# Sixteen weight loads moved from SyncE's to GpSimd's DMA queue, and nine small transpositions issued before the copy out of their tile, in a two-layer decoder step

## The chip, the cores and the metric

The kernel runs on one core of one Trainium2 chip. The metric is device time in microseconds of one execution. PE is TensorE, DVE is VectorE, ACT is ScalarE, POOL is GpSimd, SP is SyncE, which here does nothing but issue DMAs.

## The reference

One inference step of a two-layer decoder, for a prompt of 2048 tokens and 8 samples of 4 tokens that share the weights. Layer 0 is gated linear attention (GLA). Then one set of keys and values is projected, and layer 1 is grouped-query attention over a sliding window of 128 positions with sinks and a SiLU gate. The part of layer 1 that matters here:

```python
def swa_query(h, norm_g, w_in, q_norm_g, pos):
    q, gate = jnp.split(rmsnorm(h, norm_g) @ w_in, [BRANCH_WIDTH], axis=-1)
    q = rope(rmsnorm(q.reshape(bsz, seq_len, B_HEADS, B_HEAD_DIM), q_norm_g), pos)
    return q, gate

def attend(q, k, v, qpos, kpos, sinks):       # per block of 128 queries, 256 keys
    s = jnp.einsum('bqgrd,bkgd->bgrqk', qg, k) * (B_HEAD_DIM ** -0.5)
    s = jnp.where(mask, s, -jnp.inf)
    m = jnp.maximum(jnp.max(s, axis=-1, keepdims=True), sink)
    p = jnp.exp(s - m)
    p = p / (jnp.sum(p, axis=-1, keepdims=True) + jnp.exp(sink - m))
    o = jnp.einsum('bgrqk,bkgd->bqgrd', p, v)

def swa_out(o, gate, w_out):
    return (o.reshape(bsz, seq_len, BRANCH_WIDTH) * jax.nn.silu(gate)) @ w_out
```

The model width is 1024, the branch width 2048, with 32 heads of 64 in 4 groups. All is float32; the kernel writes each operand as the sum of two float16 parts and multiplies in three passes (high by high, high by low, low by high).

## The kernel before, in words

**The loop of layer 1.** For each of 4 groups and each of 16 chunks of 128 positions there is one block (class `BBlk`, 64 blocks, numbered 0 to 63). PE projects its queries (24 matmuls `pj<-W,uT`) and its gate (24 matmuls `tr<-W,uT`), forms scores (`o` and `lev` from `gl,X`) and values (`kv<-gl,sth` and `kv<-gl,pst`). Between these stand:

- the query path: POOL rotates (L1139 to L1141, `kT` at L1183), ACT and DVE split into float16 (`qe`, L194 and L195), SP transposes by DMA (`X<-qe`, L1237), and the scores read `X`;
- the score path: DVE masks and takes the maximum (L1273), ACT exponentiates (L1278), ACT and DVE split (`v`, L197 and L198), SP transposes by DMA (`sth<-v`, `pst<-v`, L1281), and the value products read `sth` and `pst`;
- the weights of the softmax on POOL (L1301, L1304, `sg` at L1308), and the result: DVE `wraw<-kv,sg` (L1317), POOL `ogT` (L195), SP stores it (`oge<-ogT`, L629).

The order of PE is fixed by hand. Each turn of the loop follows a string in which `A` is a part of the scores of the next block, `B` a part of the values of this one, and `f` a share of other work (projections of a block three turns ahead, and after the last of them products of the last stage):

```python
ORDER = "AffffffffBfAfffffffAfffAfBffff"
```

The order on the other engines is worked out when the kernel is built, by a scheduler with costs of its own, so an edit in one place can change it in others. Each engine works in its order and stands where an input or a buffer is missing; SP's and POOL's DMA issues stand in those orders too.

**The samples.** The 32 sample tokens of each group are worked in small steps (class `SampleB`) between the blocks. One of them, `norm_2`, has a PSUM tile `pQ` of nine slots. It transposes the keys into slot 8, DVE copies that slot out (`sK`, L1414), PE transposes eight pieces of the queries into slots 0 to 7 (`tr<-idh,ke`), and ACT copies those.

**The last stage.** The output projection takes the 16 chunks as 8 pairs (class `Pair`), and each pair needs seven products instead of eight, with sums of inputs and of weights. The seven weight factors were formed earlier, stored by POOL (L878) into DRAM (`wf`, seven of them), and are loaded back in quarters of 128 x 2048 float16, 512 KB each: factors 0, 2, 1, 6 by `wform_big` (L1529) into the one of four `uT` buffers, 3, 4, 5 by `wform` (L1534) into four of twelve `W` buffers. Factors 3, 0 and 2 are loaded 14, 7 and 4 blocks before the last block's projections end. Factors 1, 4, 5, 6 go into a list `trickle`, of which one item is issued with every third share of fill, around the last blocks. Their buffers held the last blocks' inputs: factors 4 and 5 take the eight `W` buffers of the fourth group's query and gate weights, factor 1 an input's `uT` buffer, and factor 6 one that the first pairs' sums read.

The first pair's inputs come back by transposing DMAs (L1565: `bt`, `S`, `qe` and others from `oge`), DVE forms their sums and differences (L1579, L1591, L1596, L1597, L1605, and splits at L195), PE multiplies (`pj`, `o`, `tr`), and for each half chunk SP loads the residual `E<-hd` (L1621), DVE adds it (L1622) and the product (`st`, L1614), and SP stores. Between the first pairs stands the samples' output: products `lev<-ogTs,uT` and `lev<-ogTs,W`, of which ACT and DVE make `ssg` (DVE at L657), which PE transposes (`tr<-idf,ssg`, L104).

Of the kernel before, what the change touches and what calls it, by code (L numbers as in the profile page):

```python
# [29 lines left out]
GRP = 8  # L30
# [44 lines left out]
def _body(tc, nc, cp, sb, ps, dr, i, o):  # L75
    uniq = [0]

    def nm(s):
        uniq[0] += 1
        return f"{s}_{uniq[0]}"  # L80

    def T(tag, shape, dt, bufs=None):
        return sb.tile(shape, dt, tag=tag, name=nm(tag), **({} if bufs is None else {"bufs": bufs}))

    def PT(tag, shape, dt=F32, bufs=1):
        return ps.tile(shape, dt, tag=tag, name=nm(tag), bufs=bufs)

    def C(tag, shape, dt):
        return cp.tile(shape, dt, tag=tag, name=tag)
# [3 lines left out]
    def order(x):  # L93

        if pin[0] and pin[1] is not None:
            tc.add_manual_dep(x.ins, pin[1].name, mybir.DependencyInfo(mybir.DependencyClass.NoSync, mybir.DependencyReason.DATA), reason="order")
        pin[1] = x.ins
        return x
# [4 lines left out]
    def tp(*a):  # L103
        return order(nc.tensor.transpose(*a))  # L104
# [12 lines left out]
    idh = C("idh", [P, P], F16)  # L117
# [28 lines left out]
    wfd = [dr.tile([P, 8, 2, 512], F16, tag=f"wf{n}", name=f"wf{n}") for n in range(7)]  # L146
# [1175 lines left out]
    class SampleB:  # L1322
# [22 lines left out]
        def steps(self):  # L1345
            g, N = self.g, SMP
# [61 lines left out]
            def norm_2():  # L1408
                Qh, KK = bx["Qh"], bx["KK"]
                pQ = PT("tr", [P, GRP + 1, N], F16, bufs=2)  # L1410
                pK = pQ[:, GRP, :]
                tp(pK, KK.rearrange("p a d -> p (a d)"), idh[:N, :N])
                Kn = bx["Kn"] = T("sK", [P, N], F16, 1)
                dve.tensor_copy(Kn, pK)  # L1414
                for h in range(GRP):
                    tp(pQ[:, h, :], Qh[:, h, :, :], idh[:N, :N])
                Q1 = bx["Q1"] = T("sq1", [P, NS, GRP, TS], F16, 1)
                act(Q1, pQ[:, :GRP].rearrange("p r (b t) -> p b r t", t=TS), AF.Copy)

# [67 lines left out]
            def att_3(tq):  # L1487
# [14 lines left out]
                split((smo[0][:, g * 4 : g * 4 + 4, 0, tk], smo[0][:, g * 4 : g * 4 + 4, 1, tk]), of)  # L1502

            return [norm, square, norm_k, norm_q, split_q, norm_2, norm_3, cache, cache_2] + [lambda tq=tq, f=f: f(tq) for tq in range(2) for f in (att, att_2, att_3)]


# [16 lines left out]
    def wform_big(n, x, box={}):  # L1523

        if x == 0:
            t = box[n] = T("uT", [P, 8, 2, 512], F16, 4)
            wf[n] = lambda k, hl, s=ALL: t[:, k, hl, s]
        ks = slice(2 * x, 2 * x + 2)
        nc.sync.dma_start(box[n][:, ks], wfd[n][:, ks])  # L1529

    def wform(n, x, ts={}):

        t = ts[n, x] = T("W", [P, 2, 2, 512], F16, NW)
        nc.sync.dma_start(t, wfd[n][:, 2 * x : 2 * x + 2])  # L1534
        wf[n] = lambda k, hl, s=ALL: ts[n, k // 2][:, k % 2, hl, s]

    quarters = lambda f, n: [lambda x=x: f(n, x) for x in range(4)]
# [143 lines left out]
    for t in range(-3, NKV * NCH):  # L1681
        fill = []
        n = t + 3
# [41 lines left out]
        if n in (TOT - 7, TOT - 4):  # L1725
            run(quarters(wform_big, {TOT - 7: 0, TOT - 4: 2}[n]))
        if n == TOT - 14:
            run(quarters(wform, 3))
        if n == TOT - 1:
            trickle += [lambda x=x: pairs[0].load(x) for x in (3, 2)] + quarters(wform_big, 1)  # L1730
            summing += pairs[0].sums()
        if n == TOT:
            trickle += quarters(wform, 4) + quarters(wform, 5)
        if n == TOT + 1:
            trickle += quarters(wform_big, 6)
# [5 lines left out]
    for p_ in range(NCH // 2):  # L1741
# [8 lines left out]
        if p_ in (3, 4):  # L1750
            n = p_ - 3
# [88 lines left out]
```

## Time and profile before

| what | us |
|---|---|
| median of 3 runs | 2842.6 |
| the three runs | 2847.57, 2840.77, 2842.6 |
| the profiled execution | 2852.25 |
| its span in the trace | 2850.1 |
| PE busy, share of the span | 2726.6, 96% |
| DVE, ACT, POOL busy | 1845.2, 1441.0, 1065.3 |
| mean granted clock of PE | 0.986 of full speed |

The span runs from the first to the last instruction of the trace; the execution's own time is 2.15 us longer. PE's busy time counts matmuls also where they run at a lower granted clock. In rows of the timeline the columns are start in us, duration in us, engine, line, operation, what is written and read, shape, how many of a kind stand there, and in brackets how long the engine had stood idle before and on what it waited. `SPq` is SP's queue of issues; the duration there is that of the issues, not of the transfer.

### The profile page before, as it was taken

How to read it: one execution, taken by the hardware profiler on the slowest of the kernel's cores; microseconds unless marked ns; L12 is line 12 of the kernel's file. 1: busy time of each engine (PE TensorE's matmuls, PEld its weight loads, DVE VectorE, ACT ScalarE, POOL GpSimd, SP SyncE). 2: the span in 40 equal slices, each digit the busy share in tenths (PEclk: the TensorE clock that was granted, in tenths of full speed). 3: DMA queues.
4: the chain of work that ended last, by engine and by line, in shares of the span. 5: the costliest groups of instructions: out<-in, count | busy, mean ns of one | idle time of the engine just before them, and what ended most of it. 6: DMA issues, size and time to landing. Idle time of an engine off the chain costs nothing.

```text
span 2850.1 us, 51664 instructions
## 1 busy us (share of the span) xinstructions
PE 2726.6 (96%) x19070; PEld 1388.6 (49%) x19070; DVE 1845.2 (65%) x3815; ACT 1441.0 (51%) x3385; POOL 1065.3 (37%) x1471
## 2 busy tenths in 40 slices
PE   6899999999999999999899999999999999979999
PEld 3444444444454444445344555555555555544444
DVE  5767778668768775435512665677767767777653
ACT  6655666556556654433312555566666666641110
POOL 1242223222322221115504686566657657530000
PEclk9999999999999999999999999999999999999999
DMA  8451325123412432799977677956867779798651
GB/s 210 90 125 36 101 86 167 34 85 122 130 38 82 153 107 74 182 227 289 243 172 182 116 146 127 213 115 131 177 125 130 144 165 177 151 210 173 135 119 57
DMA packets 795606, 395.04 MB, mean 139 GB/s; under 512 B 647504, under 2 KB 721176, under 8 KB 795320
## 3 DMA queue, kind: packets, MB, share of 16 engines
q1 hardware_dynamic: 782392, 356.01, 55.5%
q0 software_dynamic: 10880, 35.66, 3.5%
q8 instruction: 149, 2.44, 0.4%
q14 instruction: 105, 0.86, 0.1%
q10 hardware_dynamic: 2080, 0.07, 0.0%
HBM read 144.28 MB, written 107.54 MB: 88 GB/s over the span
## 4 chain that ended last, share of the span: by engine, by line
PE 57%; DVE 12%; DMA 11%; ACT 8%; issue 7%; POOL 4%; SPq 1%; ACTq 0%; DVEq 0%; POOLq 0%
PE pj L101 33%; PE o L101 10%; PE tr L101 9%; PE kv L101 3%; DMA pre<-pst 2%; DMA wraw<-in_a_w_in_dram 2%; ACT o L1278 2%; PE lev L101 1%; DVE v L198 1%; ACT v L197 1%; DVE o L1273 1%; POOL ogT L195 1%; DMA pst<-v 1%; DMA uT<-ogT 1%; DVE W L198 1%
## 5 line engine op out<-in xcount | busy, mean ns | idle before, releaser
L101 PE MATMUL pj<-W,uT 128*128 128x512 f16 x5088 | 1203.4, 383 | 7.6 <-DVE sg L478 3.0
L101 PEld LDWEIGHTS <-uT 128*128 128x128 f16 x6976 | 653.3, 98 | 717.4 <-issue 40.6
L101 PE MATMUL tr<-W,uT 128*128 128x512 f16 x1536 | 365.6, 379 | 0.0
L186 POOL TENSOR_SCALAR rs_m<-ss 128x1 f32<-128x1 f32 (+3 forms) x190 | 45.6, 240 | 683.2 <-ACT og L611 235.9
L101 PEld LDWEIGHTS <-X 128*128 128x128 f16 x2744 | 184.6, 98 | 145.9 <-issue 14.8
L1278 ACT ACTIVATE o<-o,mx 128x256 f32<-128x256 f32 (+1 forms) x384 | 168.6, 439 | 167.2 <-DVE mx L1273 163.2
L101 PE MATMUL pj<-uT,W 128*128 128x512 f16 (+1 forms) x912 | 186.5, 355 | 28.7 <-DMA uT<-ogT 24.7
L1273 DVE CUSTOM_DVE_ANT_0 o<-o,madd,nsink 128x256 f32<-128x256 f32 (+1 forms) x384 | 183.9, 479 | 46.4 <-PE o L101 42.2
L187 POOL TENSOR_TENSOR rs_r<-rs_m,mhalf 128x1 f32<-128x1 f32 (+2 forms) x186 | 185.7, 999 | 14.4
L198 DVE SCALAR_TENSOR_TENSOR v<-o,v 128x512 f16<-128x512 f32 (+1 forms) x192 | 128.8, 671 | 95.6 <-ACT v L197 93.9
L101 PEld LDWEIGHTS <-W 128*128 128x128 f16 x2448 | 128.3, 98 | 115.9 <-issue 21.5
L101 PEld LDWEIGHTS <-v 128*128 128x128 f16 x976 | 95.1, 98 | 119.5 <-DMA v<-ogd 4.3
L508 POOL TENSOR_TENSOR E<-bt 128x256 f32<-128x256 f32 x96 | 73.1, 762 | 198.7 <-DVE X L195 118.7
L195 POOL TENSOR_TENSOR ogT<-og,ogT 128x512 f16<-128x512 f32 x68 | 88.1, 1295 | 155.5 <-ACT ogT L194 150.8
L101 PEld LDWEIGHTS <-sg 128*128 128x128 f16 x800 | 78.6, 99 | 104.8 <-DMA sg<-ogd 9.4
L101 PE MATMUL o<-gl,X 128*128 128x256 f16 (+1 forms) x768 | 113.9, 271 | 6.6 <-DMA gl<-KVd 2.8
L197 ACT ACTIVATE v<-o 128x512 f16<-128x512 f32 (+1 forms) x192 | 111.2, 579 | 3.6
L1278 ACT ACTIVATE lev<-lev,mx 128x256 f32<-128x256 f32 (+1 forms) x128 | 56.5, 441 | 104.8 <-DVE mx L1273 102.8
L101 PE MATMUL pj<-W,v 128*128 128x512 f16 x448 | 104.2, 379 | 4.3 <-DMA v<-ogd 3.5
L195 DVE TENSOR_TENSOR X<-E,X 128x512 f16<-128x512 f32 x128 | 94.2, 736 | 13.4 <-ACT X L194 13.0
L248 POOL DMA_DIRECT2D pre<-pst x72 | 50.4, 701 | 139.9 <-DVE pst L198 128.4
L194 ACT ACTIVATE X<-E 128x512 f16<-128x512 f32 x128 | 79.5, 621 | 44.4 <-PE lev L101 20.6
(468 smaller groups left out, 5028.4 us busy)
## 6 DMA issues: line engine op xcount, KB each, us to landing
pre<-pst POOLq DMA_DIRECT2D x72, 256.0 KB, 3.5
W<-pre SPq DMA_DIRECT2D x36, 512.0 KB
ogd<-ogT SPq DMA_DIRECT2D x68, 256.0 KB
wraw<-in_a_w_in_dram SPq DMA_DIRECT2D x64, 256.0 KB
wraw<-in_b_w_in_dram SPq DMA_DIRECT2D x64, 256.0 KB
oge<-ogT SPq DMA_DIRECT2D x64, 256.0 KB
wraw<-in_a_w_out_dram SPq DMA_DIRECT2D x32, 256.0 KB
X<-in_x_prompt_dram SPq DMA_DIRECT2D x32, 256.0 KB
```

What stands on the lines that cost most here:

```text
L101: return order(nc.tensor.matmul(*a, **k))
L186: pool.tensor_scalar(m[:n, :k], ss, a, b, ALU.mult, ALU.add)
L187: pool.tensor_tensor(r[:n, :k], m[:n, :k], mhalf[:n, :k], ALU.pow)
L194: act(hi, src, AF.Copy)
L195: eng.tensor_tensor(lo, src, hi, ALU.subtract)
L197: act(hi, src, AF.Copy, scale=sc)
L198: dve.scalar_tensor_tensor(lo, src, sc, hi, ALU.mult, ALU.subtract)
L248: nc.gpsimd.dma_start(self.pre[:, :, half * 512 : half * 512 + 512], t)
L508: pool.tensor_tensor(Ev[:, :, 0, :], ref, btv[:, :, 0, :], ALU.subtract)
L1273: dve.tensor_tensor_reduce(pm[:, z], pm[:, z], madd.rearrange("p a b -> p (a b)")[:, (2 - nk) * P :], -0.125, nsink[:, g * GRP + h : g * G ...
L1278: act(pm[:, z], pm[:, z], AF.Exp, scale=-1.0, bias=nm_[:, h : h + 1], accum_out=bx["sum"][:, h : h + 1])
```

## The change

Sixteen DMA issues go to POOL's queue: the quarters of factors 1 and 6 (L1529) and of 4 and 5 (L1534). In `norm_2` the eight transpositions of the queries are written before the copy of the keys, so that PE no longer has a DVE read of the same tile between its writes. PE's own order around `norm_2` stays as it was.

```diff
                 tp(pK, KK.rearrange("p a d -> p (a d)"), idh[:N, :N])
+                for h in range(GRP):
+                    tp(pQ[:, h, :], Qh[:, h, :, :], idh[:N, :N])
                 Kn = bx["Kn"] = T("sK", [P, N], F16, 1)
                 dve.tensor_copy(Kn, pK)
-                for h in range(GRP):
-                    tp(pQ[:, h, :], Qh[:, h, :, :], idh[:N, :N])
...
-        nc.sync.dma_start(box[n][:, ks], wfd[n][:, ks])
+        (nc.gpsimd if n in (1, 6) else nc.sync).dma_start(box[n][:, ks], wfd[n][:, ks])
...
-        nc.sync.dma_start(t, wfd[n][:, 2 * x : 2 * x + 2])
+        (nc.gpsimd if n > 3 else nc.sync).dma_start(t, wfd[n][:, 2 * x : 2 * x + 2])
```

The scheduler's orders move with it. On SP, around the last block, the piece from the values of block 62 to the first pair's inputs (numbers behind names count tiles; `v_30679` and `v_30757` are splits of block 62's scores, `qe_30665` the last block's queries, `qe_30699` an input of the first pair, `W` and `uT` the weight factors):

```order
 L1281 DMA_TRANSPOSE pst_30627<-v_30615 128x8x128
+L1281 DMA_TRANSPOSE sth_30691<-v_30679 128x8x128
 L629 DMA oge_125<-ogT_30657 512x1x256
+L1281 DMA_TRANSPOSE pst_30769<-v_30757 128x8x128
 L1565 DMA_TRANSPOSE S_30698<-oge_114 128x8x128
 L1237 DMA_TRANSPOSE X_30668<-qe_30665 128x8x128
-L1281 DMA_TRANSPOSE sth_30691<-v_30679 128x8x128
 L1565 DMA_TRANSPOSE qe_30699<-oge_114 128x8x128
-L1529 DMA uT_30755<-wf_130 128x2048 x2
-L1281 DMA_TRANSPOSE pst_30769<-v_30757 128x8x128
-L1529 DMA uT_30755<-wf_130 128x2048 x2
-L1534 DMA W_31098<-wf_134 128x2048
```

The five loads at its end are gone from SP, seven more (L1534) are gone from a little earlier, and two transpositions of scores now stand ahead of `X` rather than behind it.

On POOL twelve of the loads now stand between the last blocks' steps. The last seven of them, and what is behind (`es` and `ogT` belong to blocks before, `kT_30580` is the last block's rotation):

```order
+L1534 DMA W_31030<-wf_134 128x2048
 L1139 TENSOR_TENSOR kT_30580<-qT_30578,bt_29905 128x512
 L1140 TENSOR_TENSOR S_30581<-qT_30578,bt_29905 128x8x32
 L1141 TENSOR_TENSOR S_30581<-qT_30578,bt_29905 128x8x32
+L1534 DMA W_31084<-wf_134 128x2048
 L1301 TENSOR_TENSOR es_5081_30718<-mx_30481,nsink 128x8
+L1529 DMA uT_30755<-wf_130 128x2048 x4
+L1534 DMA W_31098<-wf_134 128x2048
 L195 TENSOR_TENSOR ogT_30657<-wraw_30655,ogT_30657 128x512
 L1183 TENSOR_TENSOR kT_30580<-kT_30580,S_30581 128x512
```

Ahead of these stand five more (factor 4's four and the first of factor 5) between `dn` (L1304) and `rs_m` (L186); factor 6's four stand later, ahead of the next-to-last `sg` (L1308).

On DVE, the piece where the first pair's sums begin (`wraw_30784` reads the transposed inputs `S` and `qe`; `v` are splits of scores, `st` the first output, `E_31002` a sum of the second half):

```order
+L198 SCALAR_TENSOR_TENSOR v_30797<-lev_30798,v_30797 128x512
+L1614 SCALAR_TENSOR_TENSOR st_30883<-pj_30778,E_30880 128x512
+L1306 RECIPROCAL rv_30932<-dn_30930 128x8
+L198 SCALAR_TENSOR_TENSOR v_30820<-o_30821,v_30820 128x512
+L1579 TENSOR_TENSOR E_31002<-uT_28462 128x512
 L1579 TENSOR_TENSOR wraw_30784<-S_30698,qe_30699 128x512
 L1579 TENSOR_TENSOR wraw_30786<-bt_30710,bt_30711 128x512
 L1317 SCALAR_TENSOR_TENSOR wraw_30858<-kv_30726,sg_30282 128x512
-L198 SCALAR_TENSOR_TENSOR v_30797<-lev_30798,v_30797 128x512
```

Five operations that stood behind the first sum stand ahead of it.

And further on, where the samples' output is taken (`lev_31100` is its product, `E_31092` a residual):

```order
 L195 TENSOR_TENSOR sg_31139<-wraw_31135,sg_31138 128x512
 L195 TENSOR_TENSOR sg_31139<-wraw_31273,sg_31138 128x512
+L657 SCALAR_TENSOR_TENSOR ssg_31278<-lev_31100,ssg_31278 128x128
 L1622 TENSOR_TENSOR E_31092<-E_31092,Sh_30991 128x512
-L657 SCALAR_TENSOR_TENSOR ssg_31278<-lev_31100,ssg_31278 128x128
+L1317 SCALAR_TENSOR_TENSOR wraw_31337<-kv_31247,sg_30674 128x512
 L1614 SCALAR_TENSOR_TENSOR st_31095<-pj_30995,E_31092 128x512
```

`ssg` now stands ahead of the sum that waits for a load.

## The prediction

> **What bounds the kernel now.** The profiled execution took 2852.25 us (span 2850.1), 9.65 us or 0.34% above the median 2842.6. I form differences on its trace and take them off the median: 2842.6 is the base, 2852.25 is where the rows come from.
>
> I read the busy shares of the page first, then tables by window, then waits and single rows, because the change touches two kinds of place: four spots inside the long attention loop, and the 70 us in which it hands over to the last stage. The columns of a window are us, PE busy (instructions), granted clock, DMA share, GB/s.
>
> ```profile
> PE 2726.6 (96%) x19070; PEld 1388.6 (49%) x19070; DVE 1845.2 (65%) x3815; ACT 1441.0 (51%) x3385; POOL 1065.3 (37%) x1471
> ...
> 1500.00:2280.00 780.00, 767.92 (x6391) 1.00 0.71 145
> 2500.00:2520.00 20.00, 17.35 (x141) 0.99 1.02 239
> 2520.00:2540.00 20.00, 16.50 (x130) 0.93 1.04 256
> ```
>
> PE is busy 96% of the whole and 767.92 of 780 us in a long piece of the loop: what PE waits there is paid one to one. Around 2500 the picture turns. PE loses 2.65 and 3.5 us in two windows, the clock falls to 0.93, and the DMA engines are full (1.02, 1.04). The waits of PE name who is late, first over the whole span for the transpositions, then from 2260 to 2640 (total, times, longest, in us).
>
> ```profile
> PE tr L104 <- DVE sK L1414: 4.7, 4, 2.1
> ...
> PE kv L101 <- DMA pst<-v: 6.1, 5, 2.8
> PE lev L101 <- DVE v L198: 4.6, 1, 4.6
> PE tr L104 <- DVE ssg L657: 3.6, 1, 3.6
> ```
>
> So the change aims at 4.7 us in the loop, and at a handover where 2.8 (a transposing DMA), 4.6 (DVE's split of the last scores) and 3.6 us (DVE's `ssg`) stand one behind another.
>
> **The transpositions.** Nothing is added: nine PE operations keep their order, and the eight no longer wait for the DVE copy between them. Two of the four places:
>
> ```profile
> 1966.30 0.35 PE L104 MATMUL tr<-idh,ke 32*128 32x32 f16 x8 [2.10 <-DVE sK L1414]
> 1966.57 1.03 PE L101 MATMUL o<-gl,X 128*128 128x256 f16 x4
> 1967.40 4.88 PE L101 MATMUL pj<-W,uT 128*128 128x512 f16 x16
> ...
> 2195.63 0.34 PE L104 MATMUL tr<-idh,ke 32*128 32x32 f16 x8 [2.10 <-DVE sK L1414]
> 2195.91 0.61 PE L101 MATMUL o<-gl,X 128*128 128x256 f16 x4
> 2196.35 3.62 PE L101 MATMUL pj<-W,uT 128*128 128x512 f16 x16
> ```
>
> All of the 4.7 goes, since the copy's result is read by DVE's norm long after. The near bound is 4.7. The far one is 6.4: behind the stall at 1966 the next twenty matmuls took 1.03 + 4.88 against 0.61 + 3.62 behind the equal stall at 2195, 1.7 us more. One of two equal stalls was followed by slow matmuls, so the link is not certain: I take 4.7 and leave 1.7 to a rival. The Trainium skill ("TensorE: Matmul & The Clock Gate", section "Part 1: The HAM clock gate (the "warmup" mystery)") has the clock fall only after at least one idle window of about 3.4 us, which would make both stalls cost 2.1 and the sum 4.7; the slow rows behind 2.10 us at 1966 do not fit it, those at 2195 do.
>
> **The loads.** Sixteen DMA issues of 512 KB (8 MB in all) leave SP's queue for POOL's. The queue that they leave:
>
> ```profile
> 2509.87 1.48 SPq L1534 DMA_DIRECT2D W<-wf  x3
> 2511.92 2.83 SPq L1281 DMA_TRANSPOSE pst<-v  x1
> 2526.01 1.82 SPq L1237 DMA_TRANSPOSE X<-qe  x1
> 2529.22 1.33 SPq L1565 DMA_TRANSPOSE qe<-oge  x1
> ...
> 2511.92 8.18 DMA pst<-v
> 2529.22 5.86 DMA qe<-oge
> ```
>
> The first four rows are SP's issues, the last two are links of the chain: from issue to the next step 8.18 us for `pst` and 5.86 for `qe`, each with weights ahead of it or beside it. What PE and DVE make of that:
>
> ```profile
> 2520.15 0.82 PE L101 MATMUL kv<-gl,pst 128*128 128x64 f16 x12 [2.81 <-DMA pst<-v]
> 2522.47 0.82 PE L101 MATMUL o<-gl,X 128*128 128x256 f16 x4
> 2555.09 0.80 PE L101 MATMUL lev<-ogTs,uT 128*128 128x64 f16 x16 [4.55 <-DVE v L198]
> ...
> 2565.60 7.00 PE L101 MATMUL o<-uT,ke 128*128 128x512 f16 x20
> ...
> 2526.50 0.69 DVE L198 SCALAR_TENSOR_TENSOR v<-o,v 128x512 f16<-128x512 f32 x1 [0.99 <-ACT v L197]
> 2535.17 0.69 DVE L1579 TENSOR_TENSOR wraw<-S,qe 128x512 f32<-128x512 f16 x1 [5.52 <-DMA qe<-oge]
> 2538.18 0.69 DVE L1614 SCALAR_TENSOR_TENSOR st<-pj,E 128x512 f32<-128x512 f32 x1
> 2553.20 1.23 DVE L1579 TENSOR_TENSOR wraw<-uT 128x512 f32<-128x512 f16 x1
> 2554.36 0.68 DVE L198 SCALAR_TENSOR_TENSOR v<-lev,v 128x512 f16<-128x512 f32 x1
> 2563.82 0.69 DVE L1622 TENSOR_TENSOR E<-E,Sh 128x512 f32<-128x512 f32 x1 [4.41 <-DMA E<-hd]
> ```
>
> DVE serves in order. It stands 5.52 us for the `qe` tile of the first pair's sums, then works without a gap that I could find up to `v<-lev` at 2554.36, and PE, which arrived at 2555.09 - 4.55 = 2550.54, waits for that. The lever is thus DVE's time up to `v<-lev`.
>
> *How much earlier `qe` lands, x.* Bounds. Up to +5.5, the whole wait. Down to -8.1: the five loads that the new order puts just ahead of the last `kT` (factor 1's four and factor 4's or 5's last) all overtake it; a load alone takes 524,288 B / 325 GB/s = 1.61 us by the window below. My value is built from the chain of issues. Without the weights ahead of it `pst` is there when PE asks, which frees 2.81 us of stall and 1.3 of the slow clock behind it (0.07 x 20 us of the window 2520 to 2540), together 4.1: the scores of 2522.47 come at 2518.4. Their split `v` ended 4.7 behind them (2526.50 + 0.69 - 2522.47), now at 2523.1. Then SP issues `pst`, `S` and `X`, 1.3 us each as the row of `qe` shows, and `qe` at 2523.1 + 3.9 = 2527.0 to 2527.1 rather than 2529.22. x = 2.1, nearer to the middle than to either end.
>
> *Work moved from behind that wait.* The new DVE order puts five operations ahead of the waiting sum (two splits `v`, one `st`, one reciprocal, one sum `E`), and the 1.23 us sum at 2553.20 behind `v<-lev`. By the rows' starts the latter is 1.16 (2554.36 - 2553.20); the three 512-wide f32 operations count 0.6 each (a 0.69 row lets the next one start after 0.6), the split behind the reciprocal 0.56, the reciprocal 0.11. Together 3 x 0.6 + 0.56 + 0.11 + 1.16 = 3.6. They fill idle time, provided their inputs are there (those come from PE, 4.1 us earlier than now).
>
> So `v<-lev` ends 2.1 + 3.6 = 5.7 earlier and PE passes at 2549.4. PE's own way there was 2550.54, less 4.1 = 2546.4: DVE still decides, and gain is 5.7, not more. The smaller stalls between (PE on `pst`, on sums, on `v`) turn into waits for `X` and `lev`: late next is `X`, the last block's queries.
>
> *`ssg`.* Before, `ssg` stood behind `E`, which waited 4.41 us for its load; PE waited 3.6 for `ssg`. Now `ssg` goes first and the wait for `E` stands behind it, with only `st` and a value product after. 3.6 gone (bounds: 0, if the load only holds up what comes behind, as below, and 3.6). The slow matmuls after it (7.00 us for twenty) I leave as they are.
>
> *POOL.* What it pays, and what its issues cost there (min, median, max in ns):
>
> ```profile
> 2508.20 0.20 POOL L186 TENSOR_SCALAR rs_m<-ss 128x8 f32<-128x8 f32 x1 [4.08 <-DVE ss L1176]
> 2514.86 1.28 POOL L1183 TENSOR_TENSOR kT<-kT,S 128x512 f32<-128x512 f32 x1
> 2556.44 1.04 POOL L1308 TENSOR_TENSOR sg<-sg,rv 128x512 f32<-128x512 f32 x1 [0.74 <-DVE rv L1306]
> ...
> L878 POOL DMA_DIRECT2D wf<-pst x14: 539/557/587, 1293.2 to 1400.3; - x14
> L1534 SPq DMA_DIRECT2D W<-wf x12: 371/526/2149, 2276.9 to 2534.9; - x12
> ...
> 2511.22 1.89 PE L101 MATMUL tr<-W,uT 128*128 128x512 f16 x8
> ...
> 2512.00:2516.00 4.00, 4.00 (x23) 1.00 0.97 325
> ```
>
> Sixteen issues x 0.56 = 8.9 us; a store of half the size is the nearest row, so 0.53 (SP's own load) to 1.1 (twice the store, if bytes count). Twelve stand ahead of the last block's `kT`. Five of them fit the 4.08 us of idle time ahead of `rs_m`; each waits there for its buffer, and behind it wait the reciprocal roots, the rotation and so `X`. The buffers are weights of group 3, the last of them read at 2511.22 + 1.89 = 2513.1, those of the first five some microseconds earlier, since the last eight matmuls read only the last of them. The seven behind cost 3.9: `kT` at 2518.8, ACT and DVE split it, `X` could be issued by about 2524, against 2525.7 above: covered by the chain `v`, `pst`, `S`. At 1.1 each the seven cost 7.7 and `X`, then `qe`, would be 2 us late: inside the bounds of x. The last four (factor 6) stand ahead of `sg` at 2556.44; that has some ten us before a value product reads it. On SP sixteen issues fall away, which enters x and nothing else. PE's swap of two last-stage products of the first pairs moves equal matmuls: 0.
>
> Sum: 4.7 + 5.7 + 3.6 = 14.0. From 2842.6: **2828.6**, say 2829 (on the profiled execution 2838.2). With the ends of x alone: 4.7 + 3.6 + (3.6 + 2.1 + 3.4) = 17.4 down to 4.7 + 3.6 + (3.6 - 8.1) = 3.8; with half of either likely, this case's own range is 2825 to 2834.
>
> **Rivals.**
>
> *All covers hold and the clock stays up.* x = 5.5 (3.4 more), the twenty `o` matmuls at the loop's 3.62 / 16 = 0.226 us take 4.5, not 7.00 (2.5), and the 1.7 at 1966 goes too: 14.0 + 7.6 = 21.6, 2821. For it: each of the slow rows follows a stall that goes. Against it: part of the slow clock here comes behind waits that stay.
>
> *The loads overtake the transposes.* On a queue of their own nothing holds the five loads back behind `X` and `qe` any more: x = -8.1, gain 3.8, 2839. For it are rows from the middle of the kernel, where POOL's stores ran beside SP's transposes, with POOL's queue over 1379 to 1387 (packets, MB, share of the engines):
>
> ```profile
> 1382.98 1.04 PE L101 MATMUL pj<-W,sg 128*128 128x512 f16 x2 [4.43 <-DMA sg<-ogd]
> 1387.54 4.02 PE L101 MATMUL pj<-W,sg 128*128 128x512 f16 x9 [3.53 <-DMA sg<-ogd]
> ...
> q0 software_dynamic: 400, 1.31, 50.9%
> ```
>
> 1.31 MB of POOL's held half of the engines, and PE waited 4.43 and 3.53 for transposes. Against it: there SP's loads were in the mix too, and the weights moved here partly start earlier than on SP. The Trainium skill ("DMA: Bandwidth & Descriptors", section "Queues, rings and completion order") says that each engine takes turns between its queues packet by packet. By that rule POOL's large packets slow the transposes without any place in SP's order, and a time like 2839 follows; the two rows above agree.
>
> *It ends slower.* The same mechanism at full size: five transposes in a row (`sth`, `pst`, `S`, `X`, `qe`) each come about 4.0 late, the mean of 4.43 and 3.53, while 16 x 1.61 = 26 us of loads pass. `qe` then lands 20 us later than 2535.2, `v<-lev` 20 - 3.6 = 16.4, less 3.6 and 4.7: +8.1, 2850.7. It turns into a loss where `qe` lands behind 2535.2 + 3.6 + 3.6 + 4.7 = 2547.1. Against it: SP's transposes queue behind the same bytes today and `qe` came 5.86 after its issue.
>
> *The wait only moves*, `E`'s load taking `ssg`'s place through `st` and PE's next product, so that 3.6 stays: 2832; it lies in the first case's range.
>
> **How the numbers follow.** Forecast 0.46, the larger gain 0.13, loads overtaking 0.23, slower case 0.18. About 0.3% or 8.5 us is what a measurement can tell, so faster means under 2834.1 and slower over 2851.1. Faster: nearly all of the first (0.44) and all of the second, 0.57. Same: 0.02 + 0.23 and a bit under half of the last, 0.33. Slower: 0.10. The range 2819 to 2845 reaches past both gains and the overtaking, and leaves out most of the slower case and the best of the gains.
>
> **What would show it.** In the new profile PE's wait for `sK` is gone from the list. The sixteen loads stand on POOL at 0.55 us each, and the software queue carries 8 MB more. No wait of PE for `pst` near 2517; a new one for `X` of 2 to 4 us; DVE's wait for `qe` under 5.5; the `lev` products about 10 us earlier; `ssg` under 0.3. From the `lev` products to the end it takes the same time as now, less 3.6. Wrong would be: transposes that take longer than 6 to 8 us while q0 is busy; POOL standing at a load for a buffer, with `kT` past 2522; or the last products waiting for factor 4, 5 or 6.

## The result, and the profile after

The changed kernel takes 2859.2 us (median of four runs, 2853.5 to 2863.7) against 2841.7 for the kernel before on the same chip. The medians are 17.5 us apart; the ratio, 1.0045 with a 95% interval of 1.0024 to 1.0066, makes it slower by some 13 us where 14 less were forecast. The profiled execution took 2863.66 us, its span is 2861.8.

The page of the kernel after: PE's busy time is the same (2726.1 against 2726.6), so all of the difference is idle time; and the software queue, that is POOL's, carries 8.4 MB more.

```profile
PE 2726.1 (95%) x19070; PEld 1389.9 (49%) x19070; DVE 1844.9 (64%) x3815; ACT 1440.9 (50%) x3385; POOL 1077.5 (38%) x1487
...
q0 software_dynamic: 13184, 44.05, 4.5%
```

The same windows as before:

```profile
2500.00:2520.00 20.00, 12.66 (x101) 0.81 1.07 200
2520.00:2540.00 20.00, 5.00 (x31) 0.59 1.18 201
```

PE works 17.7 of these 40 us where it worked 33.9, the clock falls to 0.59, the DMA engines are as full as they were, and they move less: 200 GB/s where it was 239 and 256. The waits of PE from 2260 to 2660:

```profile
PE kv L101 <- DMA pst<-v: 13.0, 2, 12.1
PE o L101 <- DMA X<-qe: 11.7, 3, 7.3
...
PE kv L101 <- DMA sth<-v: 2.9, 1, 2.9
...
PE tr L104 <- DVE ssg L657: 1.8, 1, 1.8
```

Transposing DMAs on SP, which cost 6.1 and 1.1 us before, now cost 27.6 together. One wait is new, 2.9 us for `sth`; the others were there before, and are longer.

To compare kernels I cut the span at two marks on PE that all of them have: the last eight gate matmuls of the last block (2511.22 before, quoted ahead) and the first product of the samples' output (2555.09 before). The marks of the kernel after, and the end of the stretch as DVE sees it:

```profile
2507.68 1.89 PE L101 MATMUL tr<-W,uT 128*128 128x512 f16 x8
2516.92 1.03 PE L101 MATMUL o<-gl,X 128*128 128x256 f16 x4 [7.34 <-DMA X<-qe]
2539.68 0.82 PE L101 MATMUL kv<-gl,pst 128*128 128x64 f16 x12 [12.07 <-DMA pst<-v]
2572.43 0.59 PE L101 MATMUL lev<-ogTs,uT 128*128 128x64 f16 x16 [3.50 <-DVE v L198]
...
2555.29 0.69 DVE L1579 TENSOR_TENSOR wraw<-S,qe 128x512 f32<-128x512 f16 x1 [1.94 <-DMA qe<-oge]
```

| stage, us | before | after |
|---|---|---|
| start to the first sample transposition | 1702.3 | 1701.5 |
| from there to the last gate matmuls (loop) | 808.9 | 806.2 |
| to the first product of the samples' output (handover) | 43.9 | 64.8 |
| to the end | 295.0 | 289.4 |
| span | 2850.1 | 2861.8 |

The handover is 20.9 us longer; the loop gives 2.7 and the rest 5.6 back. (Runs of one kernel lie up to 1% apart, and the stretch ahead of the first sample transposition, which none of the edits is aimed at, takes 1689 to 1702 us in the profiles below. So stages tell more than spans, and the ratios below come from five rounds.)

SP's and POOL's rows show how it comes about:

```profile
2509.07 14.54 SPq L1281 DMA_TRANSPOSE pst<-v  x1
2523.78 11.10 SPq L1281 DMA_TRANSPOSE sth<-v  x1
...
2509.07 30.56 DMA pst<-v
...
2512.07 2.13 POOL L1529 DMA_DIRECT2D uT<-wf  x4
2516.27 0.53 POOL L1534 DMA_DIRECT2D W<-wf  x1 [2.08 <-DMA W<-wf]
2517.93 1.26 POOL L1183 TENSOR_TENSOR kT<-kT,S 128x512 f32<-128x512 f32 x1
```

POOL takes 0.53 us a load, as foreseen. It stands 2.08 us at the last of them for a transfer into its buffer, and `kT` starts 10.2 us behind the mark, where it was 3.6. That is not what PE waits for: DVE splits this `kT` only at 2548.15, after it has stood 14.94 us for PE's scores. But one transpose, `pst`, holds SP 14.5 us for its issue alone, with everything behind it in SP's order, and takes 30.6 us to the next step of the chain, 8.2 before. The DMA queues show why. First the kernel after, 2530 to 2538, then before, 2527 to 2530, where transposes ran alone (packets, MB, share of 16 engines):

```profile
q1 hardware_dynamic: 1012, 0.25, 97.9%
q0 software_dynamic: 277, 1.00, 30.6%
```

```profile
q1 hardware_dynamic: 2372, 0.59, 104.3%
```

By these shares a packet of a transpose (some 250 bytes) took 16 x 3 us x 1.043 / 2372 = 21 ns when alone, and 16 x 8 x 0.979 / 1012 = 124 ns beside POOL's loads. The two shares of the kernel after add up to 128%, so the records of packets overlap, and part of the 124 ns can be waiting. Both queues together moved 1.25 MB in 8 us, 156 GB/s; the transposes alone had moved 0.59 MB in 3 us, 197 GB/s, and loads with few other packets (36 of 353 under 512 B, the window of 2512 to 2516 quoted ahead) 325.

### The profile page after: what moved, and what is told of

Same layout as the page of the kernel before. It is cut to its first block, busy times and chain, and to the rows that moved or that the text cites. A ratio compares the mean times of both kernels' runs of the same rounds, so it can differ in the third digit from the quotient of the medians.

```text
span 2861.8 us, 51643 instructions
## 1 busy us (share of the span) xinstructions
PE 2726.1 (95%) x19070; PEld 1389.9 (49%) x19070; DVE 1844.9 (64%) x3815; ACT 1440.9 (50%) x3385; POOL 1077.5 (38%) x1487
## 3 DMA queue, kind: packets, MB, share of 16 engines
q0 software_dynamic: 13184, 44.05, 4.5%
## 4 chain that ended last, share of the span: by engine, by line
PE 63%; DVE 10%; DMA 10%; ACT 7%; issue 5%; POOL 3%; SPq 1%; ACTq 0%; POOLq 0%; DVEq 0%
PE pj L101 35%; PE o L101 12%; PE tr L101 11%; PE kv L101 3%; PE lev L101 2%; DMA pre<-pst 2%; ACT o L1278 1%; DVE v L198 1%; DMA wraw<-in_a_w_in_dram 1%; DMA pst<-v 1%; DVE W L198 1%; DMA uT<-ogT 1%; ACT v L197 1%; POOL ogT L195 1%; DMA wraw<-in_a_w_out_dram 1%
## 5 line engine op out<-in xcount | busy, mean ns | idle before, releaser
L186 POOL TENSOR_SCALAR rs_m<-ss 128x1 f32<-128x1 f32 (+3 forms) x190 | 46.0, 242 | 676.1 <-ACT og L611 232.3
L248 POOL DMA_DIRECT2D pre<-pst x72 | 50.3, 699 | 142.1 <-DVE pst L198 130.2
```

The lines of the kernel that those rows point to most:

```text
L186: pool.tensor_scalar(m[:n, :k], ss, a, b, ALU.mult, ALU.add)
L248: nc.gpsimd.dma_start(self.pre[:, :, half * 512 : half * 512 + 512], t)
```

## The experiments

All ratios are against the kernel before on the same chip, five rounds (the kernel after: four runs of each), with 95% intervals. The table gives the stages of each profile.

| kernel | loop | handover | to the end | ratio |
|---|---|---|---|---|
| before | 808.9 | 43.9 | 295.0 | 1 |
| after | 806.2 | 64.8 | 289.4 | 1.0045 |
| tp_only | 805.5 | 42.1 | 295.3 | 0.9996 |
| loads_only | 809.2 | 57.8 | 290.7 | 1.0052 |
| w45_pool | 806.2 | 56.6 | 292.5 | 1.0047 |
| f1_pool | 805.6 | 49.8 | 295.8 | 1.0020 |
| f6_pool | 808.2 | 43.4 | 294.5 | 0.9999 |
| all_act | 805.1 | 50.3 | 291.4 | 1.0016 |
| w45_act | 806.9 | 44.3 | 289.1 | 1.0005 |
| k1_pool | 805.2 | 65.2 | 296.3 | 1.0064 |
| w45_1k | 810.0 | 53.8 | 294.9 | 1.0038 |
| late45 | 805.8 | 37.5 | 299.6 | 0.9982 |
| spread | 806.8 | 36.6 | 293.4 | 0.9971 |
| spread_pool | 806.2 | 36.7 | 293.5 | 0.9968 |
| tp_att3 | 811.6 | 42.1 | 296.8 | 1.0011 |
| tp_att3b | 810.4 | 40.5 | 296.0 | 1.0012 |
| best | 814.5 | 36.6 | 293.7 | 1.0005 |
| spread_att3b | 812.7 | 36.7 | 293.2 | 0.9987 |

### The two parts, and the loads in portions

tp_only is the first hunk of the diff alone, loads_only the two others alone. w45_pool, f1_pool and f6_pool move one portion of the loads:

```diff
# w45_pool: factors 4 and 5
+        (nc.gpsimd if n > 3 else nc.sync).dma_start(t, wfd[n][:, 2 * x : 2 * x + 2])
# f1_pool, f6_pool: factor 1, factor 6
+        (nc.gpsimd if n == 1 else nc.sync).dma_start(box[n][:, ks], wfd[n][:, ks])
+        (nc.gpsimd if n == 6 else nc.sync).dma_start(box[n][:, ks], wfd[n][:, ks])
```

Expected of tp_only:

> Only the transpositions moved, all loads on SP. If the step of 4.7 us was right: ratio 0.9983 (2837), and PE's wait for `sK` gone. If the edit itself is at fault for the slower kernel (its new orders on DVE and SP): 1.003 to 1.006. Theory of the shared DMA engines says nothing against the 4.7.

Of loads_only:

> Only the sixteen loads moved. Theory A, POOL's large packets and SP's transposes slow one another in the same DMA engines: slower than the whole change by the 4.7 us that the transpositions bring, about 2864, ratio 1.007 to 1.008, again with waits of 10 us and more for `pst` and `X`. Theory B, the transpositions' new orders did it: 1.000 or below.

Of w45_pool:

> Only factors 4 and 5 (eight loads) on POOL. Theory A with the loss in proportion to the bytes beside the attention's transposes (eight of twelve loads): +22 x 8/12 = about +14, 2856, ratio 1.005; waits for `pst`, `sth`, `X` of 5 to 10 us. Theory B', the loss comes from the five loads that stand just ahead of the last `kT` on POOL, so that `X` is late: no loss, 0.998 to 1.001.

Of f1_pool:

> Only factor 1's four loads on POOL, ahead of the last `kT`. Theory A in proportion: factors 4 and 5 alone already cost what all sixteen do, so the first loads open the loss and these four would add +3 to +7, 1.001 to 1.0025. Theory B' (the loads ahead of `kT` hold the queries up): four issues x 0.55 = 2.2 us of POOL with slack, 1.000.

Of f6_pool:

> Only factor 6 (four loads) on POOL, issued after the last block's scores. Theory A: few transposes run beside it (the next pair's inputs, with slack), so little is lost and `ssg` comes earlier: 0.9985 to 1.000. If any load on POOL's queue costs by itself: +22 x 4/16 = +5.5, 1.002.

Measured: tp_only 0.9996 (0.9985 to 1.0006), loads_only 1.0052 (1.0034 to 1.0069), w45_pool 1.0047 (1.0032 to 1.0061), f1_pool 1.0020 (1.0005 to 1.0035), f6_pool 0.9999 (0.9986 to 1.0013). So the loads made the kernel slower, and the transpositions brought nothing that can be measured. Of the loads, factor 6, whose four are issued 44.5 us behind the mark, beside the last two transposes of the attention, costs nothing that can be measured (PE no longer waits for `ssg` there, and 4.5 us for a load `uT<-wf` instead); factors 4 and 5 cost most of it, and factor 1's four alone lengthen the handover by some 6 us. That all sixteen would cost 1.007 to 1.008, the 4.7 us of the transpositions on top, did not come. That theory B' is wrong shows in w45_pool: the ratio is 1.0047 where it has no loss, and the `X` and `pst` that are late were issued at 2497.24 and 2504.02, ahead of the last `kT` (2508.95). PE's waits in w45_pool, then f1_pool:

```profile
2512.09 1.03 PE L101 MATMUL o<-gl,X 128*128 128x256 f16 x4 [7.41 <-DMA X<-qe]
2520.84 0.52 PE L101 MATMUL kv<-gl,sth 128*128 128x64 f16 x12 [3.08 <-DMA sth<-v]
2527.20 0.82 PE L101 MATMUL kv<-gl,pst 128*128 128x64 f16 x12 [5.85 <-DMA pst<-v]
```

```profile
2510.74 0.82 PE L101 MATMUL kv<-gl,pst 128*128 128x64 f16 x12 [9.26 <-DMA pst<-v]
2529.08 1.03 PE L101 MATMUL o<-gl,X 128*128 128x256 f16 x4 [6.38 <-DMA X<-qe]
```

Two costs can be told apart by time. In w45_pool the loads are issued at the same place as on SP before (from 8.4 us ahead of the mark to 4.4 behind it; before 7.9 ahead to 3.6 behind, the eighth later); there it is the running side by side that costs. In f1_pool the four loads are issued 2.7 to 4.4 us behind the mark, before 19 to 23 behind: they overtake transposes, as the rivals had it.

### Where the 4.7 us of the transpositions went

The waits of PE in the loop (1690 to 2494), in the kernel before and in tp_only:

```profile
PE tr L104 <- DVE sK L1414: 4.7, 4, 2.1
...
PE kv L101 <- DVE wraw L1317: 2.1, 2, 1.6
```

```profile
PE kv L101 <- DVE wraw L1317: 6.8, 3, 3.1
```

The stall for `sK` is gone as forecast, and a wait of the same size has appeared for `wraw`: 4.7 + 2.1 = 6.8. It stands 86 us further on, where the samples' value products `kv<-ogT,ke` need the one PSUM tile `kv` that DVE has to read first (tp_only; a third wait there is 0.7 us):

```profile
2040.76 0.31 PE L101 MATMUL kv<-ogT,ke 128*64 128x16 f16 x4 [3.06 <-DVE wraw L1317]
...
2270.28 0.26 PE L101 MATMUL kv<-ogT,ke 128*64 128x16 f16 x4 [3.07 <-DVE wraw L1317]
```

Every profile says the same: in the six with the edit and the products in their place, `sK` is 0 and `wraw` 5.9 to 6.8; in the eight without it `sK` is 4.7 to 6.0 and `wraw` 0.2 to 2.6. DVE's own waits between the two places (first before, 1964 to 2050.8; then tp_only, 1954.6 to 2040.7) show that DVE waited 4.7 us for PE before, and no longer waits for PE at all, but longer for ACT and POOL:

```profile
DVE ss L1176 <- ACT E L1175: 6.7, 6, 1.1
DVE v L198 <- ACT v L197: 5.7, 11, 1.1
DVE o L1273 <- PE o L101: 3.6, 5, 1.6
...
DVE ssm L1464 <- PE tr L101: 0.6, 1, 0.6
DVE sq L1427 <- PE tr L104: 0.5, 1, 0.5
```

```profile
DVE ss L1176 <- ACT E L1175: 8.6, 6, 3.0
DVE v L198 <- ACT v L197: 6.6, 13, 1.1
...
DVE rv L1306 <- POOL dn L1304: 2.3, 3, 1.1
```

PE got ahead, and DVE, whose chain runs through ACT and POOL, did not. How much of the 4.7 is left the loops cannot settle: on average they take 806.0 us in the six profiles and 807.5 in the eight, and among the eight alone they range from 805.1 to 810.0. Two kernels tried, with all loads on SP, to take the new wait away by moving the products (`att_3`, which is taken from the list of sample steps at another share of fill):

```diff
# tp_att3
+                if boundary and seen == 7 and (n > TOT - NCH + 3 or boundary[0] in early):
...
+        if boundary and (n > TOT - NCH + 3 or boundary[0] not in early):
             boundary.pop(0)()
# tp_att3b: one turn is let pass first
+        if boundary and n <= TOT - NCH + 3 and boundary[0] in early:
+            ready.append(boundary[0])
+        elif boundary:
             boundary.pop(0)()
```

> Transpositions moved, all loads on SP; and for the first three sample groups the samples' value products (`kv<-ogT,ke`) run one share of fill before the next block's values instead of right behind this block's. Theory D, the 4.7 us stall for `sK` only moved to those products, which wait for DVE's `wraw` to free the one `kv` tile (6.8 us against 2.1): PE's waits for `wraw` fall under 1.5 us, the stretch from the first sample transposition to the last block's projection falls from 805.5 to about 801, ratio 0.997 to 0.9985. Theory E, PE is paced by DVE and ACT there: another wait takes its place and the stretch stays at 805 to 806, ratio as without this, 0.9995.

> As tp_only, and the samples' value products come seven shares of fill later (in tp_att3 they came seventeen shares too early for their own input, which took 9 us of new waits). Theory D, the 4.7 us moved to the one `kv` tile: PE's waits for `wraw` fall from 6.8 to under 1, no new wait for `ogT`, the stretch falls from 805.5 to 800 to 802, ratio 0.997 to 0.9985. Theory E, PE is paced by DVE there: 804 to 806 again, 0.9995.

Measured: 1.0011 (0.9998 to 1.0025) and 1.0012 (0.9996 to 1.0028), both loops longer, 811.6 and 810.4. The waits for `wraw` did vanish, and others came. In tp_att3 the place is seventeen shares earlier, not later as it was meant, and the products wait for their own input; in tp_att3b the block's next values wait for the samples' result in the same tile (first tp_att3, then tp_att3b):

```profile
PE kv L101 <- POOL ogT L195: 3.2, 3, 1.5
PE kv L101 <- ACT ogT L194: 3.1, 2, 1.6
...
PE kv L101 <- DVE skn L1508: 2.9, 5, 0.8
```

```profile
PE kv L101 <- DVE skn L1508: 10.6, 6, 4.2
```

That the saved stall turned into another wait is shown by the fourteen profiles; that the single `kv` tile is all that holds the 4.7 back (theory D) is not. Of theory E it came out that another wait takes its place, but not its stretch of 804 to 806 us.

### Is it GpSimd's queue, or any second queue, or the time?

all_act and w45_act put the loads on ACT's queue (all sixteen; factors 4 and 5), with the transpositions as before:

```diff
+        (nc.scalar if n in (1, 6) else nc.sync).dma_start(box[n][:, ks], wfd[n][:, ks])
+        (nc.scalar if n > 3 else nc.sync).dma_start(t, wfd[n][:, 2 * x : 2 * x + 2])
```

> The same sixteen loads on ScalarE's DMA queue, transpositions as before. Theory A, any second queue whose 4-KB packets share the DMA engines with SP's transposes: slower like the loads alone on POOL, 1.004 to 1.007 (ACT's own issue time, 16 x about 0.5 = 8 us, may add to it), and again waits of 5 us and more for `pst`, `sth` or `X`. Theory C, the slowing belongs to GpSimd's software queue: 0.998 to 1.001, with waits for transposes like those of before.

> The eight loads of factors 4 and 5 on ACT's queue. Theory A, a second queue of any engine slows the transposes alike: handover 53 to 58 us, ratio 1.004 to 1.006, as on POOL. Theory C, only GpSimd's software queue: 42 to 45 us, 0.999 to 1.001. All sixteen on ACT had 50.3 us with a wait of 8.2 for `X`, so something between, 48 to 52 us and 1.001 to 1.003, is likeliest.

Measured: 1.0016 (0.9998 to 1.0034) and 1.0005 (0.9984 to 1.0025). The waits are there too; `X` in w45_act:

```profile
2512.72 1.04 PE L101 MATMUL o<-gl,X 128*128 128x256 f16 x4 [9.02 <-DMA X<-qe]
```

and so is the slow mixture (w45_act, 2499 to 2512, then w45_pool, 2504 to 2522; packets, MB, share):

```profile
DMA packets 1984, 2.18 MB, mean 168 GB/s; under 512 B 1482, under 2 KB 1552, under 8 KB 1982
...
q10 hardware_dynamic: 483, 1.76, 60.8%
q1 hardware_dynamic: 1499, 0.39, 54.5%
```

```profile
DMA packets 2670, 3.16 MB, mean 176 GB/s; under 512 B 1950, under 2 KB 1950, under 8 KB 2668
...
q0 software_dynamic: 663, 2.42, 58.4%
q1 hardware_dynamic: 2005, 0.72, 47.3%
```

So a second queue on ACT, too, mixes with the transposes at 168 GB/s. But the handover is 44.3 us, not 56.6. Theory C's figures for w45_act (42 to 45 us, 0.999 to 1.001) came out, though not its waits like those of before: PE stands 9.02 us for `X`. Theory A had the wait and not the time (53 to 58), and the middle that was thought likeliest (48 to 52) did not come either; all_act's ratio lies between the two theories. Nor is it the same test on another queue. On POOL the eight loads are all issued by 4.4 us behind the mark; ACT issues six of them ahead of it, and the last two 10.9 and 12.6 us behind it (mark at 2501.81), the moment `X` has landed:

```profile
2500.59 0.33 ACTq L1534 DMA_DIRECT2D W<-wf  x1
2512.75 0.33 ACTq L1534 DMA_DIRECT2D W<-wf  x1
```

So two of the loads kept clear of the transposes ahead of `X`, as the held-back loads further down do. Whether that is all that makes ACT's queue the milder was not tried, and stays open.

Two kernels tried smaller packets: k1_pool is the kernel after with gaps of 32 bytes behind each KB of the weights in DRAM, w45_1k is w45_pool with such gaps and, in the core's memory, gaps of 8 bytes:

```diff
-    wfd = [dr.tile([P, 8, 2, 512], ...
+    wfd = [dr.tile([P, 8, 2, 528 if n in (1, 4, 5, 6) else 512], ...
...
+        t = ts[n, x] = T("W", [P, 2, 2, 516 if n > 3 else 512], F16, NW)[:, :, :, :512]   # w45_1k only
```

> The whole change, but factors 1, 4, 5, 6 lie in DRAM in rows of 1 KB with gaps, so that the same bytes come in packets of 1 KB. Theory A, turns by packet, one small packet of a transpose waiting for one large packet: the wait for each turn falls to about a quarter, the waits for `pst` and `X` from 24.7 to about 8 us, ratio 0.998 to 1.001. If the share goes by bytes or by time, not by packets: no change, 1.004 to 1.007.

> Factors 4 and 5 on POOL, with rows of 1 KB padded both in DRAM and in the core's memory, so that the same 4 MB come in four times as many packets. Turns by packet between the two queues: transposes get some four times their rate, the handover (last gate projection to the samples' output product) falls from 56.6 towards 46 us, ratio 1.000 to 1.002. Sharing by bytes or by time: 54 to 60 us, ratio 1.004 to 1.006. POOL's issues may get longer (to 1.0 us each).

Measured: 1.0064 (1.0041 to 1.0087) and 1.0038 (1.0021 to 1.0056). They settle nothing. POOL's queue shows as many packets as without gaps, (13184 - 10880) / 16 = 144 a load in the kernel after and in k1_pool, (12032 - 10880) / 8 = 144 in w45_1k (10880 is the count of the kernel before, with none of these loads on POOL):

```profile
q0 software_dynamic: 12032, 39.86, 4.1%
```

The gaps did not split what the profile counts as a packet, so the condition of both expectations was not met. Whether smaller packets would be kinder was not tried in another way.

The last question is time. late45 keeps all loads on SP, but makes factors 4, 5 and 6 wait, in SP's order, for the last block's transposes; spread lets each of factors 4's and 5's loads stand behind the transpose that is the last one issued when its turn comes; spread_pool does the same on POOL, with a real wait:

```diff
# spread, on top of tp_only
+                last_pt[0] = nc.sync.dma_start(pt.rearrange("p a h n q -> p (a h n) q"), ...   # L1281
...
+        ld = nc.sync.dma_start(t, wfd[n][:, 2 * x : 2 * x + 2])
+        if n > 3:
+            tc.add_manual_dep(ld.ins, last_pt[0].ins.name, ...NoSync..., reason="order")
# spread_pool: nc.gpsimd for n > 3, and Sync. late45: factors 4, 5, 6 all one turn later
```

> Transpositions moved, all loads on SP, and the loads of factors 4, 5 and 6 put behind the last block's last transpose on SP (they are first needed some 25 us later). If weights that run among the attention's transposes are what costs PE the 1.5 to 2.8 us waits for `pst` and DVE the wait for `qe`, on SP too: 0.995 to 0.998. If those waits come from the transposes' own length: 0.9985 to 1.000. If the loads then come late for their products: over 1.001, with a wait of PE for `W` or `uT`.

> All loads on SP, transpositions moved, factors 4 and 5 held back as in best, the samples' value products where they were. From the stages measured so far: 1693 + 805.7 + 36.6 + 293.7 = 2829 span against 2836 to 2841 of kernels with the usual places, ratio 0.996 to 0.9975. If the gain of the handover is given back behind it, as in late45: 0.998 to 0.9995.

> As spread, but the held-back loads of factors 4 and 5 are issued on POOL, each with a real wait for the transpose it stands behind; factors 1 and 6 on SP. Theory A', a load costs the handover what it takes alone wherever it overtakes transposes, and its queue does not matter: handover 36 to 41 us as in spread, ratio within 0.1% of it. Theory C, GpSimd's queue itself slows transposes: handover 45 us and more, ratio 1.000 to 1.004, again with transposing issues of 5 us and more on SP.

Measured: late45 0.9982 (0.9965 to 0.9999), spread 0.9971 (0.9955 to 0.9987), spread_pool 0.9968 (0.9954 to 0.9982). With the loads out of the transposes' way the handover takes 36.6 and 36.7 us, 5.5 less than in tp_only, on either queue. late45 has 37.5 there and gives 4.3 us back behind it: its twelve loads go in one burst, and PE then waits 5.1 us for an input of the second pair, `sth<-oge`, which none of its expectations had. PE's waits from 2500 to 2640 in spread_pool:

```profile
PE tr L104 <- DVE ssg L657: 3.2, 1, 3.2
PE o L101 <- DVE v L198: 2.5, 1, 2.5
PE lev L101 <- DVE v L198: 2.2, 1, 2.2
PE tr L101 <- ACT X L194: 1.8, 1, 1.8
PE kv L101 <- DMA pst<-v: 1.1, 1, 1.1
```

Waits for transposes are down to 1.1 us. POOL's eight loads are issued 32 to 51 us behind the mark there, and land in 4.4 to 9.2 us; in the kernel after, eight of the same kind took 4.6 to 23.5.

Two kernels put both ideas together, best (tp_att3 with spread) and spread_att3b (tp_att3b with spread):

> All loads on SP; transpositions moved, the samples' value products moved as in tp_att3, and factors 4 and 5 held back behind the transposes of the block that is being worked when their turn comes, which spreads them over the last two blocks (in late45 all of them and factor 6 stood in one burst, and the second pair's inputs came late by 5.1 us). Handover 38 to 41 us, the rest not longer than 295, ratio 0.993 to 0.996. If holding them back only moves the waits: 0.998.

> Both together. If both theories hold: 1693 + 801 + 36.6 + 294 = 2825, ratio 0.994 to 0.996. If only the spread loads help: 0.996 to 0.9975.

Measured: 1.0005 (0.9993 to 1.0017) and 0.9987 (0.9971 to 1.0003). The handover is as in spread, the loop loses what tp_att3 and tp_att3b lose, and both fall short of the 0.993 to 0.9975 that was expected. spread and spread_pool, 8 to 9 us faster than the kernel before, are the versions to keep.

## Why the prediction was wrong

- **The transpositions, 4.7 us.** The stall went; the sentence "all of the 4.7 goes" failed, since what stood behind the stall was never looked at. PE then waits 4.7 us more for `wraw`. The net is 0.9996 (0.9985 to 1.0006). The forecast had taken a loop with PE at 98% as one in which PE alone sets the pace.
- **The loads, x = +2.1.** This is the step that decided it: "Without the weights ahead of it `pst` is there when PE asks". The weights were no longer ahead of it in SP's line, but they ran beside it in the DMA engines, and PE stood 7.3 us for `X`, 2.9 for `sth` and 12.1 for `pst`. From the mark, DVE's first sum with `qe` came at 2535.17 - 2511.22 = 24.0 us before and at 2555.29 - 2507.68 = 47.6 after: 23.7 later, where I wrote 2.1 earlier and bounded it at 8.1 later. The bound was too near because it let loads pass at 325 GB/s and counted only the five that overtake; mixed, they ran at 156 to 176.
- **DVE's moved work, 3.6.** This held in the main: from the first sum with `qe` to the first `lev` product it took 2555.09 - 2535.17 = 19.9 us before and 2572.43 - 2555.29 = 17.1 after, 2.8 less (19.9 in tp_only, which keeps the loads on SP). With 23.7 - 2.8 = 20.9 the whole growth of the handover is accounted for.
- **`ssg`, 3.6.** PE's wait for it fell from 3.6 to 1.8, half of the term. The stretch from the `lev` products to the end is 5.6 shorter all the same, where 3.6 were forecast, partly by luck: the twenty matmuls behind, which the forecast left as they are, took 4.48 us for 7.00.
- **POOL, nothing.** The loads cost 0.53 to 0.65 us each, as said. `kT` started at 2517.9, where 2518.8 was forecast, but that is luck: the trace after runs 3.5 us ahead, and from the mark it is 10.2 us against 7.6, of which POOL stood 2.1 at a load for its buffer. It cost nothing, since DVE came for it later still.
- **The rivals.** "It ends slower" had the mechanism, and nearly the size: `qe` 20 us later where it came 23.7 later from the mark, +8.1 us against +12.8 by the ratio. How it came by the size was luck: not five transposes were 4 us late each, but `X` alone held PE up by 7.3 us and `pst` by 12.1. I gave it 0.18, and "the loads overtake" 0.23 with too small a price. What I set against both, that SP's transposes queue behind the same bytes today, is what the runs refute: in line the same stretch (2505 to 2535) moved 252 GB/s, mixed it moved 200, and 156 to 176 where the mixture was densest.

The rule of the Trainium skill quoted ahead ("DMA: Bandwidth & Descriptors", section "Queues, rings and completion order") had the direction right. It does not give the size: in the profile's count, whose packets need not be those of the page, transposes and loads passed 1012 to 277, not one for one, and a transpose's packet took six times as long as alone.

## What to carry to other kernels

A large load that stands in line between small transposes that PE waits for looks like the thing to move to another queue, but its place in line was its brake. On GpSimd's queue the loads overtook the transposes or ran beside them, and either lost time (a handover of 49.8 us with factor 1's four, 56.6 with the eight of factors 4 and 5, 43.9 before); on ACT's queue the eight cost nothing that can be measured, two of them being issued later. Ask first when the data is needed, and hold the load back until the transposes are through; then SP's queue and GpSimd's did equally well (0.9971 and 0.9968 here). And before a stall in a loop is booked as a gain, look for the next place where the same engine meets the engine it waited for.

## What the runs showed of the hardware

- A packet of a transposing DMA took six times as long beside plain loads from POOL's queue (21 to 124 ns by the shares above, waiting included). The mixture ran at 156 to 176 GB/s with POOL's queue and at 168 with ACT's, where loads with few other packets moved 325 and transposes alone 197.
- Beside POOL's loads a transpose can hold the engine that issues it: the issue of one took SP 14.5 us, of another 11.1, where the median of all is 1.2, and all that stands behind it on SP comes late.
